# A decoder trunk on eight cores: instruction order from a build-time list scheduler, and output projection, norms and next-layer inputs in token halves

**Chip, cores, metric.** One Trainium2 chip, all 8 cores, two sequences per core, no communication between cores. The metric is device time in microseconds of the slowest core. A program on all eight cores has a slow state in some executions (the cores of one die at a lower granted clock); everything below compares fast executions only, and stage lengths come from the profiled fast execution's slowest core unless another core is named.

## The reference

Four layers pass over each core: two sequences times (retention layer, forgetting-attention layer, "Fox" below). Cut to what matters:

```python
for i in range(DEPTH):                        # 2 layers: retention, forgetting attention
    h = rmsnorm(x, g_pre_mix[i])
    proj = h @ w_in                           # retention: q|k|v|gate|memory-q   Fox: q|k|v|forget|memory-q
    # retention: rotary on q and k, 6 heads of 128, chunks of 128 tokens with a carried state,
    #            per-head norm, times silu(gate)
    # Fox:       12 heads of 64, causal softmax with a cumulated log forget gate
    mem_out = memory_attention(mq, mem, ...)  # 4 heads on 256 normed memory tokens
    x = x + rmsnorm(concat(self_out, mem_out) @ w_out[i], g_post_mix[i])
    h = rmsnorm(x, g_pre_mlp[i])
    u = relu(h @ w_up[i])
    x = x + rmsnorm((u * u) @ w_down[i], g_post_mlp[i])
```

x is 2048 tokens by 1024, kept in SBUF as fp32, transposed (channels on partitions), in four token blocks of 512. Matmuls are bf16.

## The kernel before

The program order of each engine is the order in which Python calls emit instructions; semaphores come from tracked reads and writes. Overlap is made by hand: a list of deferred closures, a counter that calls `t2`, `add` and `tr` so many steps later, and "three fill steps after each chunk".

```python
def rope_steps(name, h, b, dst, dstR):            # q or k of one head, one token block
    for k in range(NCH):
        mm(pb[:], wu[:, k, :], hT[:, k, bsl(b)], ...)          # projection, 8 matmuls
        if k % 2 == 1 and k < NCH - 1:
            yield                                              # a piece to fill a gap with
    raw, rawR = rawr.next()
    act(raw, pb[:], AF.Copy, [pR], [rawR])
    swp, sR = swpr.next()
    S.add("sp", ... dma_start(swp halves <- raw halves swapped))
    t1, t1R = t1r.next()
    tt(t1, pb[:], cosT[:, bsl(b)], ALU.mult, ...)
    ...                                           # t2: swp *= sin (GpSimd), add: dst = t1 + swp
    ck.later(1, t2); ck.later(2, add)             # hand-set distances
    if name == "k":
        ck.later(5, tr)                           # four transposes on TensorE
...
# retention main loop, one chunk n of one head
    mm(ob[:, csl], v_n, a4[:, csl], ...)                       # inside the chunk
    mm(ob[:, csl], sbf, qTp[:, tsl], ...)                      # from the carried state
    mm(st_, ktok[:, n, :], v_n, ...)                           # state
    act(sbf, st_, AF.Copy, ...)                                # state to bf16
    for _ in range(3):
        next(fill, None)                                       # pieces of the next projections
    ck.tick()
...
def out_proj(l):
    for oc in range(NCH):
        for pb, pR, b in proj_unit(("out", l, oc), mixT, mR, range(NBLK), Pring):   # all 4 blocks
            ...                                    # evict, square, deferred sum of squares
    for b in range(NBLK):
        rstd_inplace(ssb[b][0], ssb[b][1], D)
    for b in range(NBLK):                          # residual tails: blocks 0, 1 now, 2, 3 deferred
        ...
# per layer: mem_kv -> norm (blocks 0 and 1 may be early) -> retention or Fox -> out_proj -> mlp
```

The softmax here doesn't subtract the row's maximum and nothing guards it: scores larger than these inputs give would overflow.

## Time and profile before

| stage (first matmul to first matmul of the next), us | retention 1 | Fox 1 | retention 2 | Fox 2 |
|---|---|---|---|---|
| head: start or end of MLP to first rope / Fox q,k | 185.1 | 156.8 | 187.2 | 156.4 |
| core: to the first output projection | 242.5 | 348.1 | 241.2 | 341.9 |
| output projection and seam: to the first up projection | 111.4 | 110.5 | 111.3 | 109.8 |
| MLP | 482 | 471 | 483 | 471.4 |

The time is 4239.61 us (median of 4 runs beside the changed kernel). If TensorE never waited and always had full clock, its matmuls would need 3272.5 us in both kernels (columns/2.4 + 2.5 ns each, the spacing in dense stretches), so 967 us are waits and lowered clock. The prediction shows the engine shares and the windows; here are the granted clock in forty slices (tenths of full speed), and three rows of TensorE's waits (waiting tile, line, the releasing engine with its tile and line: us in total, times, longest).

```profile
PEclk9898899998899997999968988999979999889998
```

```profile
PE pb L440 <- ACT scrF_s L448: 244.8, 41, 24.3
PE pb L440 <- ACT scrB_s L448: 174.0, 79, 49.3
PE pb L440 <- ACT smallb_s L448: 12.6, 6, 2.3
```

The first is TensorE waiting for the squares of a norm (the seams), the second for exponentials, squares and relus, the third for the copied retention state.

### The profile page before, as it was taken

The page shows a single profiled execution, that of the slowest core. Times are in us where ns is not written, and L with a number is a line of the kernel's source. Part 1 is how long each engine was busy: PE and PEld are TensorE (multiplying, and loading weights), DVE is VectorE, ACT ScalarE, POOL GpSimd, SP SyncE. Part 2 cuts the span into 40 slices and gives each one's busy share as a digit, 9 for nine tenths or more (in the row PEclk, how much of TensorE's full clock was granted, in tenths as well). Part 3 has the DMA queues.
Part 4 walks back from the last instruction along what each step waited for, and adds up shares of the span by engine and source line. Part 5 has one row for each costly group of instructions (what it writes and reads, how often), then busy time and mean ns, then how long its engine had stood idle before and what let it go on. Part 6 is the DMA issues. An engine that isn't in the chain of part 4 may idle for free.

```text
span 4241.3 us, 54157 instructions; the slowest of 8 cores (4214.6 to 4241.3 us)
## 1 busy us (share of the span) xinstructions
PE 3557.5 (84%) x16884; PEld 1598.2 (38%) x16884; DVE 1670.9 (39%) x2693; ACT 1668.7 (39%) x2731; POOL 788.6 (19%) x1010
## 2 busy tenths in 40 slices
PE   4687699997788996999856886999968899779996
PEld 1343244443333432444323432444424343334443
DVE  3665442313444436223145654413234444441322
ACT  3365332221467753222033653322214688432220
POOL 0144121211101102112101541212111011121211
PEclk9898899998899997999968988999979999889998
DMA  5143144444110012447431431444431100134553
GB/s 129 35 83 65 23 64 66 75 68 65 18 18 11 11 18 38 72 69 156 67 110 40 84 62 20 73 65 75 68 58 18 18 11 11 21 50 66 94 95 80
DMA packets 133268, 240.64 MB, mean 57 GB/s; under 512 B 15232, under 2 KB 19456, under 8 KB 132992
## 3 DMA queue, kind: packets, MB, share of 16 engines
q0 software_dynamic: 94176, 171.48, 26.8%
q1 hardware_dynamic: 38816, 65.69, 5.3%
q8 instruction: 147, 2.41, 0.2%
q14 instruction: 129, 1.06, 0.1%
HBM read 366.51 MB, written 16.78 MB: 90 GB/s over the span
## 4 chain that ended last, share of the span: by engine, by line
PE 73%; DVE 10%; ACT 5%; issue 5%; DMA 3%; POOL 2%; SPq 1%; DVEq 0%; ACTq 0%; POOLq 0%
PE pb L440 73%; DVE scrF_s L457 2%; DMA u2hi_s<-tab_s 2%; DVE xT_s L454 1%; ACT scrB_s L448 1%; ACT scrF_s L448 1%; ACT rl_s L448 1%; DVE rl_s L468 1%; DVE hT_s L457 1%; DMA tab_s<-tab_s 1%; POOL u2hi_s L454 1%; ACT tab_s L448 1%; DVE u2hi_s L468 1%; DMA u2hi_s<-memT 1%; SPq L565 1%
## 5 line engine op out<-in xcount | busy, mean ns | idle before, releaser
L440 PE MATMUL pb<-hT_s,wr_s 128*128 128x512 bf16 (+1 forms) x6336 | 1499.3, 387 | 58.5 <-DVE u2hi_s L454 15.6
L448 ACT ACTIVATE scrB_s<-pb 128x512 bf16<-128x512 f32 x944 | 561.5, 596 | 1651.7 <-DVE hT_s L468 820.1
L440 PEld LDWEIGHTS pb<-hT_s,wr_s 128*128 128x128 bf16 (+1 forms) x6336 | 616.7, 99 | 772.6 <-issue 127.0
L409 POOL DMA_DIRECT2D wr_s<-wall x654 | 351.7, 538 | 2319.7 <-PE pb L440 2290.0
L440 PE MATMUL pb<-mixT_s,wr_s 128*128 128x512 bf16 x3072 | 725.0, 388 | 1.6 <-POOL mixT_s L454 1.6
L468 DVE CAST hT_s<-pb 128x512 bf16<-128x512 f32 x256 | 171.0, 689 | 998.9 <-PE pb L440 998.9
L440 PE MATMUL pb<-u2hi_s,wr_s 128*128 128x512 bf16 (+1 forms) x2112 | 470.6, 380 | 14.7 <-DVE u2hi_s L457 14.7
L440 PEld LDWEIGHTS pb<-mixT_s,wr_s 128*128 128x128 bf16 x3072 | 305.9, 100 | 371.2 <-issue 33.6
L440 PE MATMUL pb<-u2hi_s 65*128 65x512 bf16 (+5 forms) x1164 | 313.2, 339 | 47.5 <-ACT scrB_s L448 35.3
L440 PE MATMUL pb<-scrF_s,cbf_s 128*128 128x512 bf16 x256 | 114.9, 502 | 248.2 <-ACT scrF_s L448 244.8
L440 PEld LDWEIGHTS pb<-u2hi_s,wr_s 128*128 128x128 bf16 x2112 | 207.2, 99 | 264.9 <-issue 21.1
L448 ACT ACTIVATE scrB_s<-pb,small_s 128x1024 bf16<-128x1024 f32 (+3 forms) x288 | 259.7, 934 | 91.3 <-PE pb L440 91.1
L454 DVE TENSOR_TENSOR u2hi_s<-scrB_s 128x512 bf16<-128x512 bf16 x256 | 111.8, 437 | 327.6 <-ACT scrB_s L448 327.6
L448 ACT ACTIVATE scrF_s<-xT_s 128x512 bf16<-128x512 f32 x256 | 139.8, 618 | 251.0 <-POOL xT_s L454 141.8
L448 ACT ACTIVATE tab_s<-pb,small_s 128x1024 bf16<-128x1024 f32 (+4 forms) x288 | 220.8, 791 | 39.2 <-PE pb L440 37.7
L440 PE MATMUL pb<-scrB_s,cbf_s 128*128 128x512 bf16 (+1 forms) x336 | 118.3, 385 | 136.4 <-ACT scrB_s L448 135.8
L468 DVE CAST u2hi_s<-pb 64x512 bf16<-64x512 f32 x192 | 132.1, 688 | 254.8 <-PE pb L440 242.9
L454 POOL TENSOR_TENSOR xT_s<-xT_s,scrF_s 128x512 f32<-128x512 f32 x128 | 162.0, 1266 | 300.7 <-DVE scrF_s L457 293.7
L454 DVE TENSOR_TENSOR mixT_s<-scrB_s 128x512 bf16<-128x512 bf16 x256 | 140.4, 552 | 195.9 <-ACT scrB_s L448 195.9
L457 DVE SCALAR_TENSOR_TENSOR hT_s<-xT_s,cst_s,rsd 128x512 bf16<-128x512 f32 x256 | 172.4, 747 | 95.9 <-ACT rsd L448 95.9
L440 PE MATMUL pb<-wr_s,hT_s 128*128 128x384 bf16 x1024 | 201.4, 343 | 6.6 <-DVE mixT_s L468 6.6
L454 POOL TENSOR_TENSOR mixT_s<-rsd,rl_s 128x512 bf16<-128x512 f32 x72 | 90.0, 1250 | 608.3 <-ACT rl_s L448 555.4
(90 smaller groups left out, 2888.9 us busy)
## 6 DMA issues: line engine op xcount, KB each, us to landing
wr_s<-wall POOLq DMA_DIRECT2D x654, 256.0 KB, 3.6
xT_s<-xT SPq DMA_DIRECT2D x8, 2048.0 KB, 23.5
outT<-xT_s SPq DMA_DIRECT2D x8, 2048.0 KB, 8.6
tab_s<-tab_s SPq DMA_DIRECT2D x96, 128.0 KB, 2.3
u2hi_s<-tab_s SPq DMA_DIRECT2D x96, 128.0 KB, 2.9
u2hi_s<-memT SPq DMA_DIRECT2D x32, 128.0 KB, 5.7
u2hi_s<-pos SPq DMA_DIRECT2D x8, 256.0 KB, 3.4
u2hi_s<-tab_s SPq DMA_DIRECT2D x24, 4.0 KB, 1.7
```

The source lines that it names most:

```text
L409: S.add("pool", (lambda d_, s_: lambda e, sem: e.dma_start(out=d_, in_=s_).then_inc(sem, 16))(dst, src), writes=[wrR[slot]], dma=True)
L440: S.add("pe", lambda e: e.matmul(out, lhsT=lhsT, rhs=rhs, start=start, stop=stop, **kw), reads=reads, writes=writes)
L448: S.add("act", lambda e: e.activation(out=out, in_=in_, func=func, **kw), reads=reads, writes=writes)
L454: S.add(eng, lambda e: e.tensor_tensor(out=out, in0=in0, in1=in1, op=op), reads=reads, writes=writes)
L457: S.add(eng, lambda e: e.scalar_tensor_tensor(out=out, in0=in0, scalar=scalar, in1=in1, op0=op0, op1=op1), reads=reads, writes=writes)
L468: S.add(eng, lambda e: e.tensor_copy(out=out, in_=in_), reads=reads, writes=writes)
L565: S.add("sp", lambda e, sem: [e.dma_start(out=memT[:, c, :], in_=memT_d[s, c]).then_inc(sem, 16) for c in range(NCH)], reads=[TM], writes= ...
```

## The change

Intent: write each stream of work (a projection, a rope, a norm, a residual tail, an attention half) as a Python generator that says what its next instruction needs; a list scheduler keeps a clock per engine with a price for each instruction and always emits, in order of rank, a stream whose next instruction can start now. And work in token halves across all seams: the output projection of tokens 0 to 1023 first, then its sums, tails and norm beside the other half's projection; the next layer's norms, memory keys and values, memory queries and v start inside the MLP and right behind it. The diff replaces most of the 1240 lines; its core, cuts marked, with a few comments of mine:

```diff
+HOP = 110.0
+SOON = 60.0
+    def run(self):                                   # class Tasks
+        while self.live:
+            now = S.avail["pe"]
+            for t in self.live:                      # sorted by rank
+                ...
+                r = S.ready(*p)                      # prices and HOP decide
+                if r <= now + SOON:
+                    best = t
+                    break
+                if best is None or r < best_r:
+                    best, best_r = t, r
+            if not self.step(best): ...
...
+    def mm(out, lhsT, rhs, start, stop, reads, writes, **kw):
+        c = max(100.0, 0.43 * n + 2) * (4 if rhs.dtype == F32 else 1)
...
-            def rope_steps(name, h, b, dst, dstR):
+    def rope(s, l, name, h, b):
+        bk = yield from ring3(s, l).acq()
+        t1 = yield from t1B.acq()                    # two buffers
+        swp = yield from swpB.acq()                  # two buffers
+        yield from group(bk, ...)                    # eight matmuls
...
-        def out_proj(l):
+    def out_half(s, l, half): ...
+    def seam_a(s, l, b): ...                         # sums, tails, norm of block b
+    def seam_b(s, l): ...
+    def seam_c(s, l): ...                            # after MLP half 0, incl. next layer's norm
+    def seam_d(s, l): ...
...
+    def mlp(s, l, mem_next):
+                if f == 10 and b == 0 and half == 0 and mem_next is not None:
+                    yield from mem_proj(*mem_next)   # next layer's memory keys and values
...
+                for blks in ((0, 1), (2, 3)):
+                    yield from mem_q(s, l, blks)
+                    if not ret and blks[0] == 2:
+                        yield from forget(s, l)
+                    yield from v_proj(s, l, blks, blks[0] == 0)
```

## The prediction

> **What bounds the kernel now.** I read the engine shares first, then the forty slices, then the matmul groups, then a table of windows that I cut at the stage boundaries seen in the timeline (slowest core, fast state).
>
> ```profile
> PE 3557.5 (84%) x16884; PEld 1598.2 (38%) x16884; DVE 1670.9 (39%) x2693; ACT 1668.7 (39%) x2731; POOL 788.6 (19%) x1010
> PE   4687699997788996999856886999968899779996
>
> ```
>
> TensorE is the bound: 84% of the span, everything else below 40%. Every dip in the second line is a place where TensorE waited, and there the granted clock dips too.
>
> I want the time that TensorE needs if it never waits. In a dense stretch 1038 matmuls of 512 columns took 224.23 us, 0.216 us each; 384 columns start 0.162 us apart, 128 columns 0.056. Counting the groups: 13,664 of 512 columns (2951 us), 1216 of 384 (197), 288 of 256 (31), about 1630 of 128 (91), a few f32 ones (9). That is a floor of about 3280 us. The span is 4241, so 960 us is idle time (684) and time at a lowered clock (the rest). Where is it? Columns: window, length, busy us of PE, weight loads, DVE, ACT, POOL, clock, DMA.
>
> ```profile
> 0.00:187.00 187.00, 103.42 (x481) 48.05 (x482) 92.16 (x174) 73.31 (x127) 10.08 (x22) 0.92 0.35 81
> 187.00:427.60 240.60, 191.93 (x1091) 90.77 (x1089) 138.93 (x193) 133.38 (x280) 109.93 (x101) 0.89 0.38 76
> 427.60:494.00 66.40, 64.81 (x289) 28.40 (x288) 22.83 (x33) 20.89 (x35) 5.43 (x9) 0.97 0.18 29
> 494.00:546.00 52.00, 13.71 (x31) 3.43 (x31) 34.94 (x47) 15.91 (x28) 12.61 (x10) 0.57 0.03 5
> 546.00:1021.00 475.00, 460.72 (x2097) 206.48 (x2096) 131.45 (x236) 119.80 (x204) 85.98 (x142) 0.99 0.46 71
> 1021.00:1076.00 55.00, 18.27 (x74) 7.34 (x75) 29.46 (x44) 17.91 (x40) 11.68 (x11) 0.54 0.19 38
> 1076.00:1178.00 102.00, 85.64 (x450) 44.05 (x448) 40.81 (x61) 41.37 (x66) 10.76 (x11) 0.96 0.12 19
> 1178.00:1524.00 346.00, 307.05 (x1535) 134.19 (x1532) 144.82 (x242) 263.63 (x334) 35.75 (x37) 0.95 0.08 12
> ```
>
> In order: start and head of the retention layer (norm, memory keys and values, rotary tables, v), its rope and core, output projection, seam to the MLP, MLP, seam to the next layer, head of the forgetting layer, its attention. The other two layers repeat this: heads 2106 to 2285 and 3131 to 3290, cores 249 and 337 us, seams 53 and 52, MLPs 477 and 463. MLPs and output projections are nearly full; seams and heads are not. One seam, in the timeline:
>
> ```profile
> 502.44 1.26 POOL L454 TENSOR_TENSOR xT_s<-xT_s,scrF_s 128x512 f32<-128x512 f32 x1 [1.35 <-DVE scrF_s L457]
> 503.06 1.19 DVE L454 TENSOR_TENSOR xT_s<-xT_s,scrF_s 128x512 f32<-128x512 f32 x1
> 517.74 4.22 PE L440 MATMUL pb<-scrF_s,cbf_s 128*128 128x512 bf16 x8 [23.82 <-ACT scrF_s L448]
> 533.46 1.10 PE L440 MATMUL pb<-scrF_s,cbf_s 128*128 128x512 bf16 x2 [11.50 <-ACT scrF_s L448]
> ```
>
> Two residual tails of about 10.5 us (four pairs of multiply and add, 2.65 us a pair), then a norm that starts only when both are through (squares 4.3, rstd 1.3, eight scalings 5.4): a serial VectorE chain with nothing for TensorE beside it.
>
> **What the Trainium skill says.** "TensorE: Matmul & The Clock Gate", What's actually happening: after an idle window of about 3.4 us the array runs at half its clock until it has been busy about as long. The trace agrees: the clock is 0.57 in the seam, and right after the wait at 427.6 six matmuls took 2.74 us against 1.46 warm. So a removed seam returns some 2 to 3 us beyond its idle time. The same page (Seeing it yourself) has a current limiter that holds a die at 13/16 of the clock under dense work on three cores; this trace differs, as dense MLP windows show 1.00, so I charge nothing for a busier TensorE. "SBUF — State Buffer", Who interferes with whom: a VectorE instruction with two SBUF inputs blocks against a GpSimd one that reads SBUF. It agrees: the tail's add takes 0.69 us alone and about 1.25 beside GpSimd. "TensorE: Matmul & The Clock Gate", Architectural detail: ScalarE and VectorE queues are strict FIFO. Hence build-time order is everything, and a misjudged duration blocks what stands behind it. No run here isolates that yet.
>
> **The change, part by part.** The arithmetic is the same, so the floor stays. Weight tiles are loaded again where a stage is split by token halves: 8 output, 2 memory-q and 6 v tiles a layer, 64 on top of 654; at 0.54 us of GpSimd issue and 3.6 us to landing this hides behind halves of 7 to 28 us.
>
> Output projection and its seam, 118 us now (66 + 52). The projection of tokens 0 to 1023 runs first; while that of the other half is on TensorE (128 matmuls, 28 us, and 16 deferred sums, 3.5 us), block 0 goes through rstd 2.6, tail 10.5, norm rest 7: about 22 us, hidden. Block 1 is done when VectorE has done both blocks (2 x 15.9 us) and the 16 evictions (11), 47 us with hops. TensorE has 28 + 3.5 + 7 us (the first four up tiles take block 0 alone), so some 9 us idle and a cold restart remain: I put 16 us beside 62 us of work. After forgetting attention about 15 us of the first half also fit into the last head pair, where no projection is left to fill. Retention 78, forgetting 63; four layers 282 against 475: **saves 193**.
>
> Heads. Memory keys and values move into the previous MLP (4.4 us of work, from a serial stretch of some 20 us). The next layer's memory-q and v for half 0 (7 + 21 = 28 us) run while blocks 2 and 3 get tails and norms (about 46 us of VectorE with v evictions), so some 17 us idle instead of 55. Forgetting head: 46, then the rest of memory-q, forget logits, v and memory attention, 47 us of TensorE, and slips: 100 each, now 157 and 159. Second retention head: each x tile is stored and reloaded before its norm (tiles of 256 KB, 2 to 4 us each way by the landing times), so block 3 is ready at about 57; then 39 us of rotary tables plus v evictions and memory divisions on VectorE bring the tables to about 117: 120, now 179. First head: x loads in tiles, so work starts near 25 us and not at 49, tables are computed meanwhile, and 80 us of TensorE work follows: 115, now 187. Sum 435 against 682: **saves 247**.
>
> Retention cores: TensorE floor 162 us (576 projection matmuls 124, 128-column work 27, head sums 10); now 241 and 249, through static filling and an unfilled last head. Every head needs 16 serial state copies, about 0.9 us a step, below the 1.7 us of work a step. I give 195 each: **saves 100**. Forgetting attention: 272 us of TensorE and 264 of ScalarE against 346 and 337. Two nearly full engines coupled through two score buffers cannot both be full: 310 each, **saves 63**.
>
> MLPs: floor 456, four stalls of about 3 us in two of them where TensorE waited for norm squares, plus the moved 4.4: 466 each, 1865 against 1878, **saves 13**. The end: stores per tile follow each add: 28 against 33, **saves 5**.
>
> Sum: 435 + 390 + 620 + 282 + 1865 + 28 = 3620. The halving, the earlier inputs and the heads carry 440 of 621.
>
> **Rivals.** (1) VectorE takes the place of the seams: the same 32 us of tails and norms per seam still has to be done, only 28 us of work is put beside it. Its 39% share speaks against a global bound, its 22.3 us busy between 125 and 150 us, in the first head, for a local one. If halves hide half of what I think, 220 us of the 440 stay: about 3840. (2) The scheduler's durations are wrong. Its cost for a 512-element f32 VectorE add is 633 ns where the groups show 683 alone and 970 on average in tails, its hop 110 ns where the timeline shows 0.2 to 0.3 us. In-order queues then stall a little everywhere: 0.15 us at each of some 1500 hand-overs is 225 us, about 3840 again. That evictions are dense and buffers doubled speaks against the full amount. (3) It goes better: if attention and cores come within 5% of their TensorE floors (285 and 170), 100 us more go: 3520. (4) TensorE being busier lowers the granted clock; for it only the skill, against it 1.00 in 450 us MLPs.
>
> **Range and chances.** I take 3620, with 3490 to 3770: (3) below and somewhat more than half of (1) or (2) above. To miss a gain of 2% (85 us), more than 530 of the 621 us must fail, and the start, four MLP seams and four layer seams are independent places. Faster 0.96, within 2% 0.025, slower 0.015.
>
> **What would show it.** TensorE share near 91%, with busy time down to about 3300 to 3350 since less of it runs at half clock; mean clock above 0.96 from 0.92; the wait of TensorE for norm squares (244.8 us in the list of waits) below 60; 64 more weight loads; seams of 10 to 20 us with VectorE busy; one long hole left, at the start of the second sequence. Wrong would be: many waits of 0.2 to 1 us in cores and attention adding to over 250 us (rival 2), seams of over 30 us with VectorE full (rival 1), or a clock near 0.81 in MLPs (rival 4).

## The result, and the profile after

3891.59 us (median of 4 runs, 3891.23 to 3893.54) against 4239.61. The ratio of fast runs is 0.9174, 95% interval 0.9149 to 0.9198. Ratios here are the mean time of one kernel's fast runs over the mean of the other's in the same rounds, so not quite the ratio of the medians. The direction is as predicted, the size is not: 348 us saved, 621 forecast, and the time is 122 us above the range's upper end.

The rows that answer to those of before, page first (engine shares, TensorE's slices, the clock):

```profile
PE 3528.7 (91%) x16884; PEld 1546.7 (40%) x16884; DVE 1608.7 (41%) x2661; ACT 1675.9 (43%) x2763; POOL 821.5 (21%) x1074
PE   6788999999899999999975889999998999999996
PEclk9999999999899999999977999999998999999998
```

TensorE's share is the 91% that the prediction named as a sign, and the dips are gone but for the start and the seam between the sequences. Two more signs came as named: 718 weight loads, 64 more, and a mean clock of 0.964 on this core (0.918 before). The 91% misled. Busy 3529 us is 256 us above the 3272.5 us of ideal work, where the prediction wanted 3300 to 3350: a lowered clock counts as busy time (about 80 us, my estimate from the trace's clock records and the columns; about 170 us before, so some 90 of the 348 us saved are clock), and so does the time of a matmul that stands alone (in the core below, 0.22 us for a 128-column matmul that takes 0.056 us in a dense stretch).

The windows at the stage boundaries of this kernel, with the columns of the prediction's table (first seven, a layer pair; the last one is the start of the second retention core):

```profile
0.00:131.00 131.00, 93.68 (x472) 42.65 (x472) 84.22 (x157) 70.39 (x132) 12.54 (x27) 0.97 0.64 131
131.00:374.70 243.70, 192.67 (x1096) 84.87 (x1097) 130.86 (x201) 137.67 (x281) 110.65 (x103) 0.96 0.37 74
374.70:451.40 76.70, 70.72 (x311) 28.21 (x310) 43.90 (x65) 35.56 (x66) 20.28 (x26) 0.99 0.45 73
451.40:933.70 482.30, 470.18 (x2162) 210.43 (x2161) 144.35 (x261) 126.52 (x222) 89.68 (x147) 0.98 0.48 72
933.70:1050.40 116.70, 99.44 (x468) 46.92 (x467) 64.44 (x97) 61.43 (x101) 25.22 (x27) 0.88 0.26 36
1050.40:1365.00 314.60, 292.44 (x1477) 122.17 (x1475) 140.07 (x227) 244.75 (x316) 34.87 (x36) 0.98 0.09 14
1365.00:1452.00 87.00, 81.80 (x371) 33.07 (x369) 46.91 (x69) 48.75 (x81) 22.46 (x27) 0.99 0.35 61
2053.00:2080.00 27.00, 7.03 (x24) 2.65 (x24) 22.52 (x45) 2.78 (x2) 0.00 (x0) 0.64 0.20 39
```

The seam (third row) is full: TensorE 70.7 of 76.7 us. In its timeline the tail of block 1 runs on VectorE and GpSimd while TensorE projects the other half:

```profile
430.87 0.74 DVE L579 SCALAR_TENSOR_TENSOR scrF_s<-hT_s,cst_s,pb 128x512 f32<-128x512 bf16 x1
...
432.57 1.89 PE L559 MATMUL pb<-mixT_s,wr_s 128*128 128x512 bf16 x8
433.27 1.26 POOL L576 TENSOR_TENSOR xT_s<-xT_s,scrF_s 128x512 f32<-128x512 f32 x1 [2.19 <-DVE scrF_s L579]
```

The retention core (second row) is as long as it was: 243.7 us against 242.5 on the slowest cores, and by the median of the eight cores 245 against 237. TensorE's waits, whole span (L944 is the transposes of k, which wait for the rope's add on VectorE):

```profile
PE pb L559 <- ACT scrB_s L567: 55.1, 98, 2.0
PE pb L559 <- ACT scrF_s L567: 42.0, 13, 16.5
...
PE pb L944 <- DVE u2hi_s L576: 33.1, 22, 3.2
PE pb L559 <- ACT smallb_s L567: 22.5, 47, 0.8
```

The norm squares fell from 244.8 to 42.0 us, as predicted (below 60). What grew is the last row: waits for the state copy, 6 before, 47 now. A look into the core shows what they are:

```profile
242.72 0.22 PE L559 MATMUL pb<-mixT_s,u2hi_s 128*128 128x128 bf16 x1
...
243.28 0.27 ACT L567 ACTIVATE smallb_s<-pb 128x128 bf16<-128x128 f32 x1
...
243.70 0.22 PE L559 MATMUL pb<-mixT_s,u2hi_s 128*128 128x128 bf16 x1 [0.65 <-ACT smallb_s L567]
...
244.01 0.28 ACT L567 ACTIVATE smallb_s<-pb 128x128 bf16<-128x128 f32 x1 [0.46 <-PE pb L559]
...
244.43 0.22 PE L559 MATMUL pb<-mixT_s,u2hi_s 128*128 128x128 bf16 x1 [0.41 <-ACT smallb_s L567]
...
244.60 1.02 PE L559 MATMUL pb<-hT_s,wr_s 128*128 128x512 bf16 x4
```

Three state steps in a row, 0.7 to 1.0 us apart, each with three short matmuls of 56 ns and nothing between: no projection was emitted there. The next one comes at 244.60. If it was a buffer that was missing when the order was made, the trace cannot name it: it shows a wait for whatever the scheduler emitted instead. The experiments below test that.

The stages against the forecast (sums over the layers; same boundaries):

| stage | before | forecast | after | after, each | miss |
|---|---|---|---|---|---|
| heads | 685.5 | 435 | 482 | 131.0, 116.7, 119.9, 114.5 | +47 |
| retention cores | 484 | 390 | 510 | 243.7, 266.6 | **+120** |
| Fox cores | 690 | 620 | 629 | 314.6, 314.6 | +9 |
| output projection and seam | 443 | 282 | 327 | 76.7, 87.0, 76.6, 86.5 | +45 |
| MLPs | 1908 | 1865 | 1911 | 482.3, 481.1, 482.2, 465.4 | +46 |
| end, after the last matmul | 31 | 28 | 32 | | +4 |

The misses sum to 271 us, which is the profiled 3892 less 3620.

### The profile page after: what moved, and what is told of

The parts are those of the page before. It is cut to its first block, busy times and chain, and to the rows that moved or that the text cites. A ratio compares the mean times of both kernels' runs of the same rounds, so it can differ in the third digit from the quotient of the medians.

```text
span 3892.0 us, 54706 instructions; the slowest of 8 cores (3883.4 to 3892.0 us)
## 1 busy us (share of the span) xinstructions
PE 3528.7 (91%) x16884; PEld 1546.7 (40%) x16884; DVE 1608.7 (41%) x2661; ACT 1675.9 (43%) x2763; POOL 821.5 (21%) x1074
## 4 chain that ended last, share of the span: by engine, by line
PE 74%; DVE 8%; ACT 8%; issue 6%; POOL 2%; DMA 1%; SPq 0%; ACTq 0%; DVEq 0%; POOLq 0%
PE pb L559 73%; ACT scrB_s L567 3%; ACT tab_s L567 2%; DVE u2hi_s L576 1%; ACT scrF_s L567 1%; DVE hT_s L579 1%; DVE scrF_s L579 1%; DVE hT_s L588 1%; ACT rsd_s L567 1%; DMA xT_s<-xT 1%; POOL mixT_s L576 1%; DVE mixT_s L576 0%; DVE xT_s L576 0%; DVE tab_s L579 0%; DMA tab_s<-tab_s 0%
## 5 line engine op out<-in xcount | busy, mean ns | idle before, releaser
L567 ACT ACTIVATE scrB_s<-pb 128x512 bf16<-128x512 f32 x880 | 521.6, 597 | 1498.1 <-DVE hT_s L588 796.7
L527 POOL DMA_DIRECT2D wr_s<-wall x718 | 387.2, 540 | 1945.4 <-PE pb L559 1912.0
L567 ACT ACTIVATE tab_s<-pb,small_s 128x1024 bf16<-128x1024 f32 (+4 forms) x288 | 223.1, 794 | 10.7 <-PE pb L559 5.7
L579 DVE SCALAR_TENSOR_TENSOR hT_s<-xT_s,cst_s,rsd_s 128x512 bf16<-128x512 f32 x256 | 173.8, 745 | 120.3 <-ACT rsd_s L567 112.2
L559 PE MATMUL pb<-wr_s,hT_s 128*128 128x384 bf16 x1024 | 187.7, 330 | 9.4 <-DVE mixT_s L588 8.3
L579 DVE SCALAR_TENSOR_TENSOR scrF_s<-hT_s,cst_s,pb 128x512 f32<-128x512 bf16 x256 | 185.8, 737 | 20.6 <-ACT pb L567 20.6
L559 PEld LDWEIGHTS pb<-u2hi_s 65*128 65x128 bf16 (+2 forms) x1164 | 102.4, 101 | 221.3 <-issue 200.5
L588 DVE COPY rl_s<-pb 64x512 f32<-64x512 f32 x96 | 66.1, 689 | 262.8 <-PE pb L559 129.9
L576 POOL TENSOR_TENSOR mixT_s<-rsd_s,rl_s 128x512 bf16<-128x512 f32 x48 | 60.8, 1266 | 513.5 <-ACT rl_s L567 376.5
L559 PE MATMUL pb<-scrB_s,scrF_s 128*128 128x512 bf16 (+1 forms) x480 | 154.6, 375 | 11.7 <-DVE rsd_s L588 11.5
## 6 DMA issues: line engine op xcount, KB each, us to landing
xT_s<-xT SPq DMA_DIRECT2D x64, 256.0 KB, 10.6
```

The lines of the kernel that those rows point to most:

```text
L527: S.add("pool", (lambda d_, s_: lambda e, sem: e.dma_start(out=d_, in_=s_).then_inc(sem, 16))(dst, src), writes=[wrR[slot]], dma=True, fre ...
L559: S.add("pe", lambda e: e.matmul(out, lhsT=lhsT, rhs=rhs, start=start, stop=stop, **kw), reads=reads, writes=writes, cost=c)
L567: S.add("act", lambda e: e.activation(out=out, in_=in_, func=func, **kw), reads=reads, writes=writes, cost=190 + 0.833 * nfree(out))
L576: S.add(eng, lambda e: e.tensor_tensor(out=out, in0=in0, in1=in1, op=op), reads=reads, writes=writes, cost=vcost(eng, out, (in0, in1)))
L579: S.add(eng, lambda e: e.scalar_tensor_tensor(out=out, in0=in0, scalar=scalar, in1=in1, op0=op0, op1=op1), reads=reads, writes=writes, cos ...
L588: S.add(eng, lambda e: e.tensor_copy(out=out, in_=in_), reads=reads, writes=writes, cost=vcost(eng, out, (in_,)))
```

## The experiments

Three views of why the cores did not shrink. Mine: the rope's two buffers each for the cosine product and the swapped copy are held from before the projection to the end of the add. In the changed kernel this is 10.6 us (from first matmul to end of add, mean of 72 ropes), a pair of ropes comes every 9.48 us, and the next-but-one rope starts within a microsecond of that end (median 0.8 us before it: the modelled clock is somewhat ahead). A round (a pair, its gate, four chunks, the head's sum) needs only 6.7 us of TensorE: 161.4 us of ideal work in a core over 24 rounds. Rival A: the scheduler's prices are too low, so in-order queues stall. Rival B: the other engines are full; the second window row speaks against it (no engine but TensorE above 57%).

The changed kernel is 3891.6. Runs e1 to e4, e5 to e8 and e9 to e12 each shared a chip and its runs of the kernel before (whose fast runs lay at 4235, 4225 to 4230 and 4229 to 4237 us); the changed kernel was measured beside a fourth set. Between these groups a difference of some 10 us is not resolved by the times alone, and I go by stages there.

**e1: a third pair of buffers.**

```diff
-    t1B = Bufs(scrF[0:2])
+    t1B = Bufs(scrF[0:2] + [rl[0]])
-    swpB = Bufs([... tabR[3]), Buf(..., swpR)])
+    swpB = Bufs([... tabR[3]), Buf(..., swpR), rl[1]])
```

> Three buffers instead of two for the rope's product with cosine and for its swapped copy (the third pair is the 128x512 fp32 pair that attention on the memory uses at other times). My theory: in the two retention cores (first rope to first output projection: 243.7 and 266.6 us after the change, where I had forecast 195 each) the next ropes wait for one of two buffers that is held from before the projection to the end of the add, about 10 us, so a third pair shortens each core by 15 to 40 us: 3820 to 3862 us. The scheduler's own clock, which knows the buffers, says 18 and 16 us. Rival A (the scheduler's hand-over of 110 ns is too short, so the in-order queues stall in small waits): buffers are not the limit, cores within 5 us, 3885 to 3897 us. Rival B (DVE, ACT and GpSimd are simply full with the core's work): also within 5 us.

3876.8 to 3902.5 us in three fast runs (ratio to before 0.9176). The profiled execution was slow on one die; core 1 on the other die has cores of 238.5 and 266.8 us. Only 5 and 0 us: as it was put, my theory failed here, and the run looks like the rivals' "within 5".

**e2: take the two buffers after the projection.**

```diff
-        t1 = yield from t1B.acq()
-        swp = yield from swpB.acq()
         yield from group(bk, ...)
         ...
         raw = yield from rawB.acq()
+        t1 = yield from t1B.acq()
+        swp = yield from swpB.acq()
```

> Still two buffers of each, but taken after the eight projection matmuls instead of before, so that each is held about 2.3 us less of some 10 us. My theory: a shorter hold works like a third buffer; cores 20 us shorter each (the scheduler's own clock: 22 and 23), 3835 to 3860 us. Rival A and rival B: cores within 5 us, 3885 to 3897 us.

3874.9 us (median; ratio to before 0.9159). Cores 236.3 and 251.9: 7 and 15 us, below the 20 forecast but not nothing.

**e3: the price of a short matmul.**

```diff
-        c = max(100.0, 0.43 * n + 2) * ...
+        c = max(56.0, 0.43 * n + 2) * ...
```

> Only the scheduler's price of a matmul of up to 128 columns is changed, 100 ns to 57 ns; the trace shows 56 ns. Same instructions, another order. My theory: with the rope's buffers as they are the retention cores hardly move (the scheduler's own clock: -1.6 and 0 us); Fox attention gains up to 14 us a layer on that clock, so 3850 to 3892 us, all of it in the Fox layers. Rival C (the 100 ns price is what holds the retention cores, because PE looks busy to the scheduler when it is free): both cores 15 us or more shorter.

3886.4 us (median of the four fast runs of five; ratio 0.9183). The Fox cores gain 9 and 11 us (305.2, 303.2); the retention cores get longer, 255.9 and 276.0. Rival C (the price alone holds the cores) falls.

**e4: both.**

> The two edits together. My theory: with the rope's cycle shortened PE becomes the next limit in the scheduler's eyes, so the right price of short matmuls now counts: cores 40 us shorter each (to about 203 and 226), 3760 to 3800 us, more than the sum of the two alone. Rival A: the order is still made with too short a hand-over, and the denser it is the more it stalls: less than 40 us in all, 3850 us or above.

3801.3 us (median; 3798.5 to 3829.7; ratio 0.8992). Cores 210.9 and 235.5, Fox 304.1 and 300.9. For the retention cores e2 and e3 alone sum to 1 us of gain; together they give 64. The wait before each kind of matmul in the first core says where it went (worked out from the start times: the gap before a matmul less its predecessor's ideal time, less the loss by clock; us):

| wait before | changed kernel | e2 | e3 | e4 |
|---|---|---|---|---|
| state and output steps | 31.7 | 10.5 | 26.5 | 6.7 |
| transposes of k | 19.4 | 27.4 | 15.3 | 15.3 |
| gate projections | 6.0 | 9.0 | 18.5 | 2.3 |
| rope projections | 9.4 | 10.7 | 6.4 | 10.1 |
| head's sum of squares | 8.4 | 4.0 | 15.7 | 10.8 |
| scores | 2.4 | 1.2 | 1.0 | 0.3 |
| sum | 77.3 | 62.8 | 83.4 | 45.5 |

The shorter hold does what I claimed, the wait at the state steps falls to a third, but under the old price transposes and gates take over a part of it; under the right price alone the buffers keep the steps bare. The rest of a core's length over TensorE's 162 us and this sum is lowered clock: about 4, 11, 10 and 3 us in the four columns, so half of what e2 gained in waits went to the clock. The profile's own rows, first core only, changed kernel, then e2, then e4:

```profile
PE pb L944 <- DVE u2hi_s L576: 16.6, 11, 3.2
PE pb L559 <- ACT smallb_s L567: 11.1, 22, 0.8
```

```profile
PE pb L944 <- DVE u2hi_s L576: 24.1, 20, 3.7
...
PE pb L559 <- ACT smallb_s L567: 2.0, 8, 0.4
```

```profile
PE pb L944 <- DVE u2hi_s L576: 11.8, 12, 2.3
...
PE pb L559 <- ACT smallb_s L567: 1.4, 3, 0.5
```

**e12: e1's third pair with e3's price.** It asks whether e4's gain came from buffers at all, or from the particular order that late taking makes.

> The third buffers of e1 together with the 56 ns price of e3, and nothing else; the buffers are taken before the projection as in the changed kernel. If a longer life of the buffers is what e4 cured, a third pair does the same with the right price: cores about 211 and 236 as in e4, 3790 to 3815 us, although e1 alone gave little (238 and 267). If e4's gain came from the order that late taking makes and not from the buffers as such, the cores stay above 230 and 255: 3850 us or above.

3800.6 us (median of four fast runs, 3798.9 to 3804.4; ratio 0.8979), within 2 us of e4; cores 216.6 and 239.4. In the list of waits of the first core, the state copy has 10.9 us in 24 places in e3 and 2.1 us in 4 in e12. Two different ways to relieve the buffers reach the same time, both only with the right price. So the buffer time is one of two conditions, and the price of the short matmul is the other. Why the greedy order needs both (with 100 ns it believes TensorE busy where it is free) is argued, not shown.

**e5: rotary tables earlier, memory keys later (on e4).** (The edit moves the memory keys from the 11th up-projection tile to the 14th.) The second core keeps 24 us more than the first. The last window row above shows its start: VectorE 22.5 of 27 us with the rotary tables, TensorE 7.0. And inside three MLPs TensorE waits for the memory norm, whose VectorE work stands behind residual tails; it comes out cold, 16 matmuls in 3.57 us:

```profile
496.53 3.42 DVE L579 SCALAR_TENSOR_TENSOR u2hi_s<-u2hi_s,cst_s,rsd_s 128x256 bf16<-128x256 f32 x6
500.10 3.57 PE L559 MATMUL pb<-u2hi_s,wr_s 128*128 128x256 bf16 x16 [5.74 <-DVE u2hi_s L579]
```

The tables also get other scratch buffers, since the tails use the old ones at that time.

```diff
-            for b in range(NBLK):            # rotary(), second sequence
+            for b in range(2):
                 yield wait("h", s, l, 0, b)
-        A, B_ = scrF[0], scrF[1]
+        A, B_ = rawB.items
...
-                if f == 10 and b == 0 and half == 0 and mem_next is not None:
+                if f == 13 and b == 0 and half == 0 and mem_next is not None:
```

> On top of e4_late_and_56ns two moves, each to be read in its own stage: the second sequence's rotary tables start once token blocks 0 and 1 have their norm instead of all four (their scratch moves to the rope's two raw buffers, since the tails use the old scratch), and the next layer's memory keys and values come before the 14th up-projection tile instead of the 11th. My theory: the 24 us hole before the first ropes of the second retention layer is the tables' VectorE chain, and the 5.7 us hole in the first three MLPs is the memory norm that VectorE reaches late behind the tails. So second core 235 to 211 us, three MLPs 482 to 477 each, 3750 to 3775 us (e4 had 3801). Rival: VectorE is full there anyway, so the head in front gets as much longer (117 to 130 or more) and the MLPs stay at 482: 3785 to 3800.

3750.6, 3754.4 and 3778.6 us (ratio 0.8896). Second core 235.5 to 215.3; its head stays at 116.8, where the rival had it longer. MLPs 473.2, 473.8, 474.9 (from 481.9, 480.7, 482.3): 8 each, more than the 5 forecast, since the clock loss goes too (3.57 us became 1.91 for those 16 matmuls).

**e6: calibrated prices (on e5).** Hand-over (HOP, the time that the scheduler allows from the end of one engine's instruction to the start of another's that needs it) 110 to 150 ns, VectorE 1.1 to 1.2 ns an element.

> e5 with the scheduler's hand-over at 150 ns instead of 110 and a VectorE fp32 element at 1.2 ns instead of 1.1, same instructions. Rival A (small waits come from prices that are too low): the waits before transposes (15 us a core in e4) and before the head's sum of squares (11 us) shrink by half, cores and Fox attention 8 us or more shorter each, 20 to 40 us below e5. My theory: prices matter little once the buffers allow the order; within 12 us of e5, either way.

3742.2 us (3740.7 to 3744.3; ratio 0.8852): some 10 us below e5's two best runs, within my band, and not what rival A wanted: seams 323 to 309, cores 214.2 and 213.8 (from 210.9 and 215.3).

**e7: hand-over 200 ns, nothing else.**

> The changed kernel with the scheduler's hand-over at 200 ns instead of 110 and nothing else. Rival A: what the trace shows (0.2 to 0.3 us) is now planned for, cores and Fox attention 10 us or more shorter each, 3850 us or below. My theory: the order is not the limit; the scheduler's own clock (3864 us) becomes honest but nothing gets shorter, 3880 to 3920 us.

3867.7 us (mean of two fast runs; ratio 0.9148): faster than the changed kernel by 24 us by the times, by 11 by the ratios (0.9174 and 0.9148, with intervals that overlap), which neither text had. Fox cores 302.7 and 305.1 (12 and 10 shorter), seams and MLPs 26 us less, but retention cores 253.5 and 282.4, 10 and 16 longer. So rival A is right for Fox, seams and MLPs (48 us in sum) and wrong for the retention cores (26 us lost): there TensorE's waits for the state copy grow to 32.8 us in 75 places. That a hand-over priced longer also holds the rope's buffers longer on the scheduler's clock would explain it; no run isolates that.

**e8: next layer's inputs late.** One line, seam_c waits for the end of the MLP before it norms blocks 0 and 1 of the next layer.

```diff
-        yield wait("up", s, l, 1)
+        yield wait("mlpend", s, l)
         if n is not None:
             for b in (0, 1):
                 yield from norm(n[0], n[1], 0, b, b, bank[6 + b])
```

> The changed kernel with one part undone: the next layer's norm of token blocks 0 and 1 waits for the end of the MLP instead of running beside its second half's down projection; what follows from it (memory queries and values of half 0) comes later too. Prices this part of the heads' saving. My forecast put a removed 38 us of idle time per head on it (17 instead of 55 us); if that holds heads of layers 2 to 4 get 30 us or more longer each, 3980 us or above. If most of it is covered anyway by VectorE work that stays in front of the head (the scheduler's own clock: heads +16, +12, +16, MLPs -4 each), 3915 to 3935 us.

3927.4 and 3928.0 us in the two fast runs: 36 us slower by the times. Heads of layers 2 to 4 become 130.5, 128.2 and 131.0 on core 0 (14, 12 and 16 longer than on core 0 of the changed kernel), the first three MLPs 3 us shorter each. My 38 us of removed idle time per head was too much for this part; the kernel before had it already, within a sequence. What else shortens the heads (memory keys moved, memory queries and v by halves) was not priced one by one.

**e9: the ones row under its own name (on e6).** The Fox head holds this, in the changed kernel:

```profile
991.06 7.03 POOL L595 MEMSET u2hi_s<- 1x2048 bf16 x4
...
998.27 0.74 DVE L584 TENSOR_SCALAR u2hi_s<-pb,cst_s 12x512 f32<-12x512 f32 x1 [6.54 <-POOL u2hi_s L595]
...
999.88 1.01 PE L559 MATMUL pb<-scrB_s,mvaug_s 128*128 128x512 bf16 x2 [6.56 <-DVE mixT_s L576]
```

Read downwards: four memsets of one partition, priced 1.12 us each, take 1.76; VectorE's bias add is booked on the same name and waits; the division behind it in VectorE's queue waits; TensorE waits for the division.

```diff
-                memset(kX[i][hh][64:65, :], 1.0, [TM], kXR[i][hh], eng="pool")
+                memset(kX[i][hh][64:65, :], 1.0, [TM], [oneR], eng="pool")
...
-                            r_ = [kXR[i][hh][kt // 4], qXR[i][hh][2 * j + q], TM]
+                            r_ = [kXR[i][hh][kt // 4], qXR[i][hh][2 * j + q], oneR, TM]
```

> On top of e6. In the Fox head four GpSimd memsets of the ones row (1x2048 each) take 7.03 us; the forget gate's bias add on VectorE is ordered behind them because both are booked under one name, although they touch other partitions, and the division of the memory attention, then TensorE, stand behind it (6.54 and 6.56 us, and TensorE goes cold). The edit books the row under its own name. My theory: the two Fox heads get 8 to 12 us shorter each (117.6 and 118.3 in e6), 3715 to 3730 us. Rival: the wait only moves to the next thing that is late there (tails of block 3): heads shorter by under 3 us each, 3735 or above.

3726.4 and 3728.4 us (ratio 0.8805, e6 0.8852), 15 us below e6 by the times, 20 by the ratios. Fox heads 108.2 and 108.3, from 117.6 and 118.3: as forecast.

**e10: the price of a transfer (on e9).** It was meant for the rope's swap, but the edited line prices every transfer, weights and x tiles too.

```diff
-                self.wire = max(t + 1800, self.wire) + nbytes / 165.0
+                self.wire = max(t + 2500, self.wire) + nbytes / 165.0
```

> On top of e9, the scheduler's latency of a transfer goes from 1800 to 2500 ns, no instruction added or removed. The rope's half swap is planned to land 3.4 us after its issue, the trace has 5.1 us from raw copy to GpSimd in the median (3.0 to 6.7). If the waits before the transposes (14.8 us a core in e6, 22 of 24 transposes) come from a swap priced too low, they shrink to a third and both cores end 8 to 15 us shorter (to about 203): 3695 to 3712 us. Rival: the rope's two buffers are held that long whatever the price, so what no longer waits at the transposes waits at the next rope: cores within 5 us, 3715 to 3730.

3701 us (3700.9 and 3701.2; ratio 0.8743), 26 us below e9. Cores 207.7 and 206.3 (from 219.8 and 215.4), seams 10 us shorter in sum, MLPs 8 us longer. TensorE's waits before the transposes in the first core, e9 and then e10 (by half, not to a third as forecast):

```profile
PE pb L944 <- DVE u2hi_s L576: 11.3, 12, 2.6
```

```profile
PE pb L944 <- DVE u2hi_s L576: 6.0, 4, 3.4
```

**e11: the transfer's price with the old other prices.**

> As e10, but with the hand-over back at 110 ns and VectorE at 1.1 ns an element, so the swap's price alone is changed on top of e5 and the ones row. The scheduler's own clock has it 45 us shorter than e10 (cores 188 and 186 against 201 and 193). If that clock is right the chip shows below 3690 us. If the higher prices are the better picture, as e6 against e5 says, the chip gives the 45 us back: 3700 to 3730 us, at or above e10.

3715.1 to 3720.6 us (ratio 0.8783). The scheduler's clock promised 45 us less than for e10, the chip took some 16 more: the retention cores are shorter (199.3 each), the seams 28 us and Fox 8 us longer in sum than in e10. As in e7 and e6, a higher hand-over (in e6 and e10 with a higher VectorE price) went with shorter seams and with retention cores that are no shorter. A lower modelled time is not a better order where the prices are off.

The fastest kernel is e10: 3701 us, ratio to before 0.8743 against 0.9174 for the change, 190 us below it by the times, 183 by the ratios.

## Why the prediction was right or wrong

**The failed step: "I give 195 each" for the retention cores.** It went from TensorE's floor of 162 us and a state chain of 0.9 us a step "below the 1.7 us of work a step", and assumed that such work is at hand to be put between the steps. It is not: the rope's buffers decide how many projections may be under way, and they are held 10.6 us for a round that needs 6.7 us of TensorE. Measured 243.7 and 266.6, +120 us of the 271 (without it the time would have been 3772 us, at the range's upper end of 3770, so the smaller misses below count too). With buffers and price both mended (e4, e12) the cores came to 211 to 217 and 235 to 239; the tables earlier (e5) brought the second to 215; the transfer's price (e10) both to about 207, and with the old other prices (e11) to 199.3 each. The forecast's 195 was nearly there to be had, but not in the kernel as written. I had the diff, and could have counted the buffers' holding time against the round.

**Rival 2 (prices).** Written as 225 us everywhere. Right in kind, wrong in size and place: the hand-over alone 11 to 24 us (e7), the short matmul alone next to nothing (e3, ratio 0.9183 against 0.9174: 21 us shorter in Fox, 22 us longer in the retention cores) but, with the buffers relieved, 74 us (3874.9 in e2 to 3801.3 in e4), the transfer's price 26 (e10; the swap's part of it is not isolated). The sign named for it, waits of 0.2 to 1 us in cores and attention adding to over 250 us, was not there: counted from the traces they add to 58 us in 130 places, against 54 us in 120 before. What the prices cost was an order with other holes, not many small stalls.

**Heads, "435".** Measured 482. The second retention head came out as predicted (119.9 for 120), but by luck: the forecast had the rotary tables done in it, and they fell into the core as the 24 us hole. The first is 131 for 115: it starts on transfers. The two windows at its start have DMA shares of 0.93 and 0.99 while TensorE is busy 2 and 16 of 25 us:

```profile
0.00:25.00 25.00, 2.11 (x4) 0.41 (x4) 12.62 (x26) 4.31 (x7) 3.02 (x9) 1.00 0.93 172
25.00:50.00 25.00, 15.53 (x40) 4.00 (x40) 10.78 (x16) 12.39 (x26) 0.53 (x1) 0.86 0.99 293
```

I took "near 25" as the start of full work. No run tests another way of loading. The Fox heads, 116.7 and 114.5 for 100, owe 10 us each to the memset (e9). The long hole at the second sequence's start is there as said, and it is a wait for x tiles reloaded:

```profile
1989.34 0.63 ACT L567 ACTIVATE scrF_s<-xT_s 128x512 bf16<-128x512 f32 x1 [10.84 <-DMA xT_s<-xT]
1990.12 0.58 PE L559 MATMUL pb<-scrF_s,cbf_s 128*128 128x512 bf16 x1 [12.30 <-ACT scrF_s L567]
```

**Output projection, seam and Fox attention.** Right for retention (76.7 for 78; of it 66 us are ideal work, where 62 were forecast, and 10.5 us waits and clock, where 16 were). For Fox the table's boundary flatters the core and blames the seam: the first output projection (1365.1) starts 17 us before the last attention matmul (1381.7), the overlap of about 15 us that I had credited. Counted to its own end, attention took 331 us in each layer for a forecast of 310, and from there to the MLP it was 70 us for 63. So of the 28 us missed in each Fox layer three quarters belong to the step "310 each". The right price of the short matmuls (e3) took 9 and 11 us off, so a part of it is rival 2; the rest stays open. No run undoes the token halves of the output projection: what they save is read from the stage table and the timeline alone.

**MLPs, "466 each".** 482 in three, 465.4 in the last, which has no memory keys to make for a next layer. The moved 4.4 us were put in at full clock with no wait; the wait of 5.7 us and the cold restart were missed. e5 got 8 of 16 us back.

**Rivals 1 and 4** were judged well: TensorE is busy through the retention seam, and the clock in MLPs is 0.98. In one place rival 1 came true: VectorE's 22.5 of 27 us at the start of the second retention core.

**Two readings.** The prediction says that the trace agrees with half the clock after an idle window of 3.4 us. That holds for the seam (a wait of 23.8 us), not for its second example: before the slow matmuls at 427.6 the two nearest waits lasted 2.2 and 0.8 us. Short waits can cost the clock too, which the forecast of the cores left out. And a head has 15 state steps, not 16, which changes little.

**The end**: 32 us for 28; the stores per tile gained no more than a microsecond.

## What to carry to other kernels

When a scheduler chooses the order, the buffers are its constraints and the durations its beliefs, and either can void a gain in the other: for each ring count the holding time per use against the round it serves, and check the price of every frequent instruction against the trace. A shortage at build time showed here only as idle steps of some other chain. A busy share can reach its forecast while the time does not; subtract the ideal work stage by stage.

## What the Trainium skill lacked or had wrong

- "TensorE: Matmul & The Clock Gate", Back-to-back issue gap: this section gives a sustained 81 ns for 128 columns and 131 ns for 512 in streams with weight loads, and calls columns/2.4 + 2.5 ns the isolated case. Here the latter holds in dense streams with a weight load for each matmul: 0.216 us for 512 columns, 0.056 for 128.
- The same page, Seeing it yourself: the 13/16 clock under dense work on three cores of a die. Here it depends on the execution: in fast ones all eight cores ran at a mean clock of 0.965, 0.98 in an MLP; in one slow execution of e7 cores 4 to 7 had 0.81 (4356 to 4384 us) while cores 0 to 3 had 0.96 (3860 to 3863 us).
- No page that I looked up says how busy TensorE has to be to keep its clock. In the profile of the kernel before, the granted clock of core 5 fell to half 71 times. Before 50 of these falls no single wait had reached 3.4 us, and before 69 TensorE was busy for less than 62% of the last 3.4 us (some such stretches, down to 42%, kept full clock). It came back 70 times, always after 3.4 us that were busy for 79% or more.
- No page that I looked up has a GpSimd memset's time: one of 1x2048 bf16 took 1.8 us on average.
- None says how much later a swap within SBUF can land beside weight traffic: in e6 the rope's transfers of 128 KB landed 2.3 us after issue in the median and 6.3 at most. From the raw copy's end to GpSimd's multiply it was 5.1 us in the median in e6, and 3.4 us in the changed kernel, so the path of a swap is more than its transfer.
